# Hybrid encoder layer on one core: the norm's g as a column, applied when transposed tiles leave PSUM, and matmuls of ones ahead of TensorE's first work

## The chip, the cores and the metric

The kernel runs on one core of a Trainium2 chip. The metric is the device time of one execution in microseconds (us). A core has five engines, each with a queue of its own that it works through strictly in order: TensorE (PE in the profile; its weight loads are shown apart as PEld), VectorE (DVE), ScalarE (ACT), GpSimd (POOL) and SyncE (SP), which in this kernel issues most of the transfers. TensorE writes to PSUM, eight banks, which ACT and DVE read; everything else lies in SBUF, 128 partitions wide.

## The reference

One layer of an encoder over x of 1024 tokens by 1024 features, in float32. What matters here is its first step and what uses it:

```python
def rmsnorm(x, g):
    y = x * lax.rsqrt(jnp.mean(x * x, axis=-1, keepdims=True) + EPS)
    return y * g

h = rmsnorm(x, g_mix)
z = h @ w_in                            # pooling channels | q | k | v
y_pool = pool_mixer(z[..., :512], w_pool_grp, pool_scale)
y_attn = diff_attention(q, k, v, ...)   # 8 heads, block-causal
gates = sigmoid(h @ w_gate + b_gate)    # 2048 columns
x = x + (gates[..., :1024] * (y_pool @ w_branch_pool)
         + gates[..., 1024:] * (y_attn @ w_branch_attn)) @ w_out
x = x + square(relu(rmsnorm(x, g_ffn) @ w_up)) @ w_down
```

g_mix has one number for each of the 1024 features. It is 1 plus 0.05 times a normal number, so it can't be left out.

## The kernel before

**Tiles.** The tokens are cut into eight tiles of 128 (t = 0 to 7, x0 to x7). A matmul contracts over the 128 partitions, so h is needed transposed: features on partitions, tokens along the row. hT holds it as eight blocks of 128 features (k = 0 to 7), for each half of the tokens (th = 0, 1), in two parts: a high part, rounded to the format that TensorE takes (float32r), and a low part, the rest. Weights are held in the same two parts. Every product is then three matmuls (`mm3`, L126 to L128: high times high, high times low, low times high), summed in one bank.

**The norm of one tile** (`norm_transpose`, L237) runs over four engines. ACT squares x and sums the rows (L252; for tile 0 ACT and DVE take a half each, L244 and L245); DVE and POOL make the factor rs from the sum (L234 and L235; tile 0: L249 and L250); DVE multiplies x by rs and by g, 512 columns at a time, into hn (L256); TensorE transposes hn, four blocks of 128 into one bank of 512 columns (L261), so that a tile fills two banks, named hps; and `split` brings a bank into hT in two steps of 256 columns each: ACT casts the high part (L120), DVE subtracts it for the low part (L121). On one bank ACT and DVE take turns: ACT's second cast waits for DVE's reading for the first. For L256 g must lie on all 128 partitions: gmb, a tile of 128 by 1024, is loaded by one transfer that repeats the row (L345).

**The order at the start.** `START` (L43) lists the first steps: x0, g, norm of tile 0, four pairs of weights of head 0 (w0 to w3, each two transfers into a tile rqkv; their casts and low parts are made on ACT, POOL and DVE), x1 and so on. SP issues the transfers in that order, all on one queue: x0 in two halves, g, eight transfers of weights, then x1, x2, x3, small parameters, x4. The projection of tile t for head h is named z (`stage_qkv`, L405): eight steps, one per block k, of three matmuls of 384 columns. The other work on TensorE at the start is the first gate block (g in the profile's names, with weights fwgate), 24 matmuls of 512 columns over the first four tiles, and transposes for the heads.

**What sets the order.** A scheduler puts the instructions of each engine in order. It goes by the order in which the code was written, as a priority, and by its own estimate of when each instruction's operands are ready; `tc.issue_after(i)` keeps what is issued under it behind instruction i. So an edit to one step moves others on all engines.

Of the kernel before, what the change touches and what calls it, by code (L numbers as in the profile page):

```python
# [17 lines left out]
P = 128  # L18
# [23 lines left out]

START = "x0 g n0 w0 w1 w2u w3u x1 s0p s1 x2 s2p s3 x3"  # L43
NX = [-2, -1, 0, 0, 0, 1, 2, 3]
# [14 lines left out]
def encoder_kernel(  # L59
# [63 lines left out]
    def mm3(ps, lhs_hi, lhs_lo, rhs_hi, rhs_lo, first, last, more=False):  # L123

        kw = {"skip_group_check": True} if more else {}
        nc.tensor.matmul(ps, lhs_hi, rhs_hi, start=first, stop=False, **kw)  # L126
        nc.tensor.matmul(ps, lhs_hi, rhs_lo, start=False, stop=False, **kw)  # L127
        nc.tensor.matmul(ps, lhs_lo, rhs_hi, start=False, stop=last, **kw)  # L128

# [106 lines left out]

    def norm_transpose(xt, gb, t, dst, hn, small, banks, halves=False):  # L237

# [12 lines left out]
        else:  # L251
            nc.scalar.activation(hn, xt, AF.Square, accum_out=ss)  # L252
            rsq(rs, ss, 1, 1.0 / D)
        for j in range(2):
            js = slice(j * 512, (j + 1) * 512)
            nc.vector.scalar_tensor_tensor(hn[:, js], xt[:, js], rs, gb[:, js], op0=ALU.mult, op1=ALU.mult)  # L256
            trp, trtag = banks[j % len(banks)]
            ps = trp.tile([P, 512], F32, tag=trtag, name=f"hps{t}_{j}")
            for i in range(4):
                k = 4 * j + i  # L260
                nc.tensor.transpose(ps[:, i * P : (i + 1) * P], hn[:, k * P : (k + 1) * P], identf)  # L261
            for i in range(2):
                kp = 2 * j + i
                src = ps[:, i * 256 : (i + 1) * 256].rearrange("p (a b) -> p a b", a=2)
                split(dst[kp, th, 0][:, :, c0 : c0 + P], dst[kp, th, 1][:, :, c0 : c0 + P], src)

# [8 lines left out]
    with ExitStack() as ph:  # L275
# [39 lines left out]
        def norm_x(t):  # L315
# [6 lines left out]
            banks = [(ps_t, "tr"), (ps_s, "sc")][: 2 if t < N_SC else 1]  # L322
            norm_transpose(xs.pop(t), gmb, t, hT, hn, sp, banks, t == 0)

# [7 lines left out]
        KV = {}  # L332
        hT = {}
        for w in START.split():
            if w[0] == "x":
# [5 lines left out]
            elif w[0] == "s":  # L341
                split_w(0, int(w[1]), nc.gpsimd if w[2:] else nc.vector)
            elif w[0] == "g":
                gmb = ut([P, D], F32, "gmb")
                nc.sync.dma_start(gmb, g_mix[0].partition_broadcast(P))  # L345

# [58 lines left out]
        def stage_qkv(h, t):  # L405
# [4 lines left out]
            for k in range(NK):  # L410
                l_hi = hT[k // 2, th, 0][:, k % 2, c0 : c0 + P]
                l_lo = hT[k // 2, th, 1][:, k % 2, c0 : c0 + P]
                w = Wh[h][k]
                mm3(z[:, 0:384], l_hi, l_lo, w[:, 0, :], w[:, 1, :], k == 0, k == NK - 1)
                yield
# [1112 lines left out]
```

## Time and profile before

| | before |
|---|---|
| median of 3 runs | 1529.52 us (1528.83 to 1530.18) |
| the profiled execution | 1529.71 us |
| its span (first to last instruction) | 1527.6 us |
| mean granted TensorE clock | 0.999 |
| instructions | 21675 |
| HBM traffic | 157.76 MB read, 61.90 MB written |

Durations below come from that one execution, so sums are made against its own 1529.71 us: the span and 2.1 us around it. In the profile, each line gives an engine, a line of the kernel, an operation and `out<-in` by the names of the tiles; a time in brackets behind "idle before" is how long the engine had waited, and for whom. The granted clock is a share of TensorE's full clock. "SPq" and "ACTq" are instructions that issue transfers. How the work spreads over the whole span is seen in the page's second part, 40 slices with busy tenths:

```profile
PE   7999999999999999999999999999999999999998
DVE  6776668777777777746578559766665668556572
ACT  6665556656565565454464466555555634333331
POOL 6687333335234242312100011000000000000000
```

A slice is 38 us long. Only the first and the last slice of PE are below 9.

### The profile page before, as it was taken

To read this page: it belongs to the slowest core of one execution; us is meant where nothing else is said; L and a number is where in the kernel's file an instruction comes from. 1 tells how busy PE (TensorE), PEld (TensorE's weight loads), DVE (VectorE), ACT (ScalarE), POOL (GpSimd) and SP (SyncE) were. 2 spreads that over 40 slices of the span, in tenths; PEclk is the share of its full clock that TensorE was granted. 3 is DMA by queue.
4 is the path that set the end of the run, shared out by engine and by line. 5 is a ranking of instruction groups with operands and counts; after the bars stand their busy time and mean duration, and the time that the engine had idled before them with its cause. 6 is when DMAs were issued, how large, how long until landed. Compare 5 with 4: busy or idle time off the path is not lost.

```text
span 1527.6 us, 21675 instructions
## 1 busy us (share of the span) xinstructions
PE 1509.7 (99%) x7441; PEld 1302.0 (85%) x7441; DVE 1048.5 (69%) x2262; ACT 804.7 (53%) x1693; POOL 319.8 (21%) x412
## 2 busy tenths in 40 slices
PE   7999999999999999999999999999999999999998
PEld 6999999999898989888888888888888888888887
DVE  6776668777777777746578559766665668556572
ACT  6665556656565565454464466555555634333331
POOL 6687333335234242312100011000000000000000
PEclk9999999999999999999999999999999999999999
DMA  7253202112112131627365734554433799537750
GB/s 247 100 159 120 76 29 62 51 44 66 43 44 84 49 98 40 223 89 254 120 209 191 248 104 149 169 178 152 148 128 110 274 344 383 170 125 262 228 190 28
DMA packets 171608, 221.07 MB, mean 145 GB/s; under 512 B 10902, under 2 KB 104811, under 8 KB 171499
## 3 DMA queue, kind: packets, MB, share of 16 engines
q1 hardware_dynamic: 154090, 192.39, 38.0%
q10 hardware_dynamic: 17408, 27.30, 4.8%
q8 instruction: 59, 0.97, 0.3%
q14 instruction: 51, 0.41, 0.1%
HBM read 157.76 MB, written 61.90 MB: 144 GB/s over the span
## 4 chain that ended last, share of the span: by engine, by line
PE 95%; DVE 2%; DMA 1%; ACT 1%; SPq 1%; issue 0%; POOL 0%; DVEq 0%
PE z L126 6%; PE z L128 6%; PE z L127 6%; PE Da L126 4%; PE Da L128 4%; PE Da L127 4%; PE g L126 4%; PE g L127 4%; PE g L128 4%; PE Db L126 3%; PE Db L128 3%; PE Db L127 3%; PE X L128 3%; PE X L127 3%; PE X L126 3%; PE sc L484 2%
## 5 line engine op out<-in xcount | busy, mean ns | idle before, releaser
L126 PE MATMUL z<-wqkv,hT 128*128 128x384 f32 x512 | 174.9, 343 | 0.6 <-DVE qn L428 0.4
L128 PE MATMUL z<-wqkv,hT 128*128 128x384 f32 x512 | 173.7, 340 | 0.0
L127 PE MATMUL z<-wqkv,hT 128*128 128x384 f32 x512 | 173.5, 339 | 0.0
L495 ACT ACTIVATE s<-s,nm 128x256 f32<-128x256 f32 (+7 forms) x128 | 99.5, 778 | 46.5 <-DVE nm L487 45.6
L126 PE MATMUL g<-hT,fwgate 128*128 128x512 f32 x256 | 101.1, 395 | 0.1
L127 PE MATMUL g<-hT,fwgate 128*128 128x512 f32 x256 | 100.8, 394 | 0.0
L128 PE MATMUL g<-hT,fwgate 128*128 128x512 f32 x256 | 100.5, 393 | 0.0
L126 PEld LDWEIGHTS z<-wqkv,hT 128*128 128x128 f32 x512 | 96.8, 189 | 3.4 <-DVE qn L428 0.6
L127 PEld LDWEIGHTS z<-wqkv,hT 128*128 128x128 f32 x512 | 96.9, 189 | 3.1 <-POOL wqkv L121 0.2
L235 POOL TENSOR_TENSOR ms<-ms,mhalf 128x4 f32<-128x4 f32 x64 | 65.7, 1027 | 158.3 <-DVE ms L234 135.3
L128 PEld LDWEIGHTS z<-wqkv,hT 128*128 128x128 f32 x512 | 96.5, 189 | 2.5 <-DVE hT L121 0.3
L121 DVE TENSOR_TENSOR AT<-ta,AT 128x256 fp32r<-128x256 f32 (+1 forms) x160 | 62.2, 392 | 32.7 <-ACT AT L120 31.6
L487 DVE CUSTOM_DVE_ANT_0 s<-sc,dist 128x512 f32<-128x512 f32 (+3 forms) x128 | 73.9, 583 | 13.2 <-PE sc L485 12.1
L120 ACT CAST AT<-ta 128x256 fp32r<-128x256 f32 (+1 forms) x160 | 54.5, 347 | 37.9 <-PE ta L527 23.1
L484 PE MATMUL sc<-K,Q 128*128 128x512 f32 (+2 forms) x192 | 69.8, 365 | 0.5 <-DVE nm L487 0.5
L121 DVE TENSOR_TENSOR AS<-s,AS 128x512 fp32r<-128x512 f32 x64 | 44.1, 693 | 36.5 <-ACT AS L120 36.3
L485 PE MATMUL sc<-K,Q 128*128 128x512 f32 (+2 forms) x192 | 66.4, 350 | 0.0
L121 POOL TENSOR_TENSOR wqkv<-rqkv,wqkv 128x384 fp32r<-128x384 f32 x60 | 61.8, 1044 | 19.8 <-ACT wqkv L120 16.7
L121 POOL TENSOR_TENSOR fwgate<-frgate,fwgate 128x512 fp32r<-128x512 f32 x32 | 43.3, 1356 | 66.0 <-ACT fwgate L120 66.0
L126 PEld LDWEIGHTS g<-hT,fwgate 128*128 128x128 f32 x256 | 48.1, 188 | 9.3 <-ACT go L730 0.5
L128 PEld LDWEIGHTS g<-hT,fwgate 128*128 128x128 f32 x256 | 48.1, 188 | 8.9
L127 PEld LDWEIGHTS g<-hT,fwgate 128*128 128x128 f32 x256 | 48.1, 188 | 8.4
(455 smaller groups left out, 4485.0 us busy)
## 6 DMA issues: line engine op xcount, KB each, us to landing
wd<-in_w_down_dram SPq DMA_DIRECT2D x56, 512.0 KB, 5.6
wu<-in_w_up_dram SPq DMA_DIRECT2D x32, 512.0 KB, 4.4
udS<-us SPq DMA_DIRECT2D x64, 256.0 KB, 2.4
ur<-udS SPq DMA_DIRECT2D x32, 512.0 KB, 3.4
rqkv<-in_w_in_dram SPq DMA_DIRECT2D x64, 192.0 KB, 2.7
ud<-u ACTq DMA_DIRECT2D x48, 256.0 KB, 4.1
ur<-ud SPq DMA_DIRECT2D x24, 512.0 KB, 4.3
frgate<-in_w_gate_dram SPq DMA_DIRECT2D x32, 256.0 KB, 2.8
```

Of the source, the lines that this page charges most:

```text
L120: nc.scalar.copy(hi, src)
L121: return (lo_eng or nc.vector).tensor_tensor(lo, src, f(hi), op=ALU.subtract)
L126: nc.tensor.matmul(ps, lhs_hi, rhs_hi, start=first, stop=False, **kw)
L127: nc.tensor.matmul(ps, lhs_hi, rhs_lo, start=False, stop=False, **kw)
L128: nc.tensor.matmul(ps, lhs_lo, rhs_hi, start=False, stop=last, **kw)
L235: nc.gpsimd.tensor_tensor(dst, dst, mhalf[:, :n], op=ALU.pow)
L484: nc.tensor.matmul(dst, Q[:, i, 0, :], rhs, start=True, stop=False)
L485: nc.tensor.matmul(dst, Q[:, i, 1, :], rhs, start=False, stop=True)
L487: nc.vector.tensor_tensor_reduce(out=s[i][:, c : c + w], in0=sc[:, 0:w], in1=dist[:, o0 + c : o0 + c + w], scale=2.0 ** -(h + 1), scalar=B ...
L495: nc.scalar.activation(s[i][:, 0:n], s[i][:, 0:n], AF.Exp, bias=last, scale=-1.0, accum_out=Z[:, i, t : t + 1])
```

## The change

g is no longer multiplied into hn. It is loaded as a tile of 8 rows by 128 (grow; ACT issues the transfer), transposed by TensorE into a bank and copied by DVE to gcol, one column of 128 for each block k. DVE's multiply makes hn from x and rs alone (`tensor_scalar`). When a transposed block leaves its bank, its features lie on partitions, so g is a number per partition: ACT's copy takes gcol as its scale and gives the high part, and DVE's `scalar_tensor_tensor` takes the bank times gcol, less the high part. This is done for each block of 128 columns apart: eight pieces on ACT and eight on DVE for a tile, where there were four and four. The large transfer of g is gone from SP's queue.

The squares of tiles 1 to 3 on ACT are held behind an earlier tile's last piece (`cast_done`: tile 0's for tiles 1 and 2, tile 1's for tile 3). And TensorE multiplies a tile of ones by itself, 512 columns, into a bank that nobody reads (idle): 16 times ahead of everything else, and 4 times behind the last matmul of z of tile 0.

```diff
-START = "x0 g n0 w0 w1 w2u w3u x1 s0p s1 x2 s2p s3 x3"
+START = "x0 n0 w0 w1 w2u w3u x1 s0p s1 x2 s2p s3 x3"
...
-        nc.tensor.matmul(ps, lhs_lo, rhs_hi, start=False, stop=last, **kw)
+        return nc.tensor.matmul(ps, lhs_lo, rhs_hi, start=False, stop=last, **kw).ins
...
-            nc.scalar.activation(hn, xt, AF.Square, accum_out=ss)
+            with ExitStack() as behind:
+                if t < 4:
+                    behind.enter_context(tc.issue_after(cast_done[0 if t < 3 else 1]))
+                nc.scalar.activation(hn, xt, AF.Square, accum_out=ss)
             rsq(rs, ss, 1, 1.0 / D)
         for j in range(2):
             js = slice(j * 512, (j + 1) * 512)
-            nc.vector.scalar_tensor_tensor(hn[:, js], xt[:, js], rs, gb[:, js], op0=ALU.mult, op1=ALU.mult)
+            nc.vector.tensor_scalar(hn[:, js], xt[:, js], rs, None, op0=ALU.mult)
...
-            for i in range(2):
-                kp = 2 * j + i
-                src = ps[:, i * 256 : (i + 1) * 256].rearrange("p (a b) -> p a b", a=2)
-                split(dst[kp, th, 0][:, :, c0 : c0 + P], dst[kp, th, 1][:, :, c0 : c0 + P], src)
+            for i in range(4):
+                k, src = 4 * j + i, ps[:, i * P : (i + 1) * P]
+                hi, lo = (dst[k // 2, th, d][:, k % 2, c0 : c0 + P] for d in range(2))
+                cast_done[t] = nc.scalar.activation(hi, src, AF.Copy, scale=gcol[:, k : k + 1]).ins
+                nc.vector.scalar_tensor_tensor(
+                    lo, src, gcol[:, k : k + 1], f(hi), op0=ALU.mult, op1=ALU.subtract
+                )
...
+        idle = ps_o.tile([P, 512], F32, tag="o", name="idle")
+
+        def keep_warm(n):
+            for _ in range(n):
+                nc.tensor.matmul(
+                    idle.rearrange("p (a b) -> p a b", a=4), ones, ones.unsqueeze(1).broadcast_to([P, 4, P]),
+                    start=True, stop=True,
+                )
+
+        keep_warm(16)
+        gcol = sp.tile([P, NK], F32, name="gcol")
+        grow = sp.tile([NK, P], F32, name="grow")
+        nc.scalar.dma_start(grow, g_mix[0].rearrange("(k p) -> k p", p=P))
+        g_ps = ps_t.tile([P, 512], F32, tag="tr", name="g_ps")
+        nc.tensor.transpose(g_ps[:, 0:NK], grow, identf[0:NK, 0:NK])
+        nc.vector.tensor_copy(gcol, g_ps[:, 0:NK])
...
-            elif w[0] == "g":
-                gmb = ut([P, D], F32, "gmb")
-                nc.sync.dma_start(gmb, g_mix[0].partition_broadcast(P))
...
-                mm3(z[:, 0:384], l_hi, l_lo, w[:, 0, :], w[:, 1, :], k == 0, k == NK - 1)
+                done = mm3(z[:, 0:384], l_hi, l_lo, w[:, 0, :], w[:, 1, :], k == 0, k == NK - 1)
+                if (h, t, k) == (0, 0, NK - 1):
+                    with tc.issue_after(done):
+                        keep_warm(4)
```

How the scheduler's order moves is seen at two places. The first is ACT's first tile: the casts of the eight weight halves of head 0 (wqkv from rqkv) and the high parts of hT of tile 0, from the banks hps0_0 (blocks 0 to 3) and hps0_1 (blocks 4 to 7). hT0 to hT3 are pairs of blocks; the next number of the name is the half of the tokens and the one after it 0 for the high part. Before:

```order
L120 CAST wqkv0_0_200<-rqkv0_0_186 128x384
L120 CAST wqkv0_1_203<-rqkv0_0_186 128x384
L120 CAST wqkv0_2_206<-rqkv0_1_189 128x384
L120 CAST hT0_0_0_150<-hps0_0_167 128x2x128
L120 CAST wqkv0_3_209<-rqkv0_1_189 128x384
L120 CAST wqkv0_4_214<-rqkv0_2_192 128x384
L120 CAST hT2_0_0_154<-hps0_1_177 128x2x128
L120 CAST hT1_0_0_152<-hps0_0_167 128x2x128
L120 CAST wqkv0_5_217<-rqkv0_2_192 128x384
L120 CAST wqkv0_6_220<-rqkv0_3_195 128x384
L120 CAST hT3_0_0_156<-hps0_1_177 128x2x128
```

And of the change, from the third weight half on:

```order
L120 CAST wqkv0_2_235<-rqkv0_1_218 128x384
L120 CAST wqkv0_3_238<-rqkv0_1_218 128x384
L120 CAST wqkv0_4_243<-rqkv0_2_221 128x384
L120 CAST wqkv0_5_246<-rqkv0_2_221 128x384
L270 ACTIVATE hT0_0_0_171<-hps0_0_188,gcol_162 128x128
L120 CAST wqkv0_6_249<-rqkv0_3_224 128x384
L270 ACTIVATE hT2_0_0_175<-hps0_1_202,gcol_162 128x128
L120 CAST wqkv0_7_252<-rqkv0_3_224 128x384
L270 ACTIVATE hT0_0_0_171<-hps0_0_188,gcol_162 128x128
L270 ACTIVATE hT2_0_0_175<-hps0_1_202,gcol_162 128x128
L270 ACTIVATE hT1_0_0_173<-hps0_0_188,gcol_162 128x128
L270 ACTIVATE hT3_0_0_177<-hps0_1_202,gcol_162 128x128
```

The first piece of hT stood behind three weight casts and stands behind six now; the pieces of the two banks alternate behind them.

The second place is PE behind z of tile 0 (z0_0; z0_1 is tile 1's). Before:

```order
L127 MATMUL z0_0_372<-wqkv0_7_223,hT3_0_0_156 128x384
L128 MATMUL z0_0_372<-wqkv0_7_223,hT3_0_1_157 128x384
L261 MATMUL hps1_0_255<-identf_96,hn1_248 128x128 x4
L261 MATMUL hps1_1_265<-identf_96,hn1_248 128x128 x4
L126 MATMUL z0_1_442<-wqkv0_0_200,hT0_0_0_150 128x384
L127 MATMUL z0_1_442<-wqkv0_0_200,hT0_0_0_150 128x384
L128 MATMUL z0_1_442<-wqkv0_0_200,hT0_0_1_151 128x384
```

And of the change:

```order
L127 MATMUL z0_0_433<-wqkv0_7_252,hT3_0_0_177 128x384
L128 MATMUL z0_0_433<-wqkv0_7_252,hT3_0_1_178 128x384
L346 MATMUL idle_145<-ones_103 128x512 x4
L266 MATMUL hps1_0_284<-identf_96,hn1_277 128x128 x4
L266 MATMUL hps1_1_298<-identf_96,hn1_277 128x128 x4
L266 MATMUL hps2_0_322<-identf_96,hn2_315 128x128 x4
L126 MATMUL z0_1_515<-wqkv0_0_229,hT0_0_0_171 128x384
```

Four matmuls of ones stand between z of tile 0 and tile 1's transposes, and half of tile 2's transposes have moved ahead of z of tile 1. On DVE the multiply of tile 3 by its factor now stands behind the making of tile 4's factor, and tile 3's transposes stand ahead of z of tile 2 on PE.

More of the change, by code (lines that the diff above doesn't have):

```diff
@@ L235, in rsq, with norm_transpose @@
         nc.gpsimd.tensor_tensor(dst, dst, mhalf[:, :n], op=ALU.pow)
-    def norm_transpose(xt, gb, t, dst, hn, small, banks, halves=False):
+    cast_done = {}
+    def norm_transpose(xt, gcol, t, dst, hn, small, banks, halves=False):
         th, c0 = t // 4, (t % 4) * P
@@ L322, in norm_x @@
             banks = [(ps_t, "tr"), (ps_s, "sc")][: 2 if t < N_SC else 1]
-            norm_transpose(xs.pop(t), gmb, t, hT, hn, sp, banks, t == 0)
+            norm_transpose(xs.pop(t), gcol, t, hT, hn, sp, banks, t == 0)
         def split_w(h, kp, eng):
```

## Prediction

> **What bounds the kernel now.** First the page's busy shares and the waits of PE over the whole span (engine, line, whom it waited for: us, times, longest).
>
> ```profile
> PE 1509.7 (99%) x7441; PEld 1302.0 (85%) x7441; DVE 1048.5 (69%) x2262; ACT 804.7 (53%) x1693; POOL 319.8 (21%) x412
> PE hps L261 <- DVE hn L256: 10.6, 2, 8.8
> ```
>
> TensorE is the bound: it is idle for 1527.6 - 1509.7 = 17.9 us, and 10.6 of these are two waits of the norm's transposes, 8.8 at the start and 1.8 later. The change works on the norm, so the question is how much of the first 43 us it can win. Second view: the windows (length, then busy us of PE, PEld, DVE, ACT, POOL, then granted clock, DMA share, GB/s).
>
> ```profile
> 0.00:8.75 8.75, 0.00 (x0) 0.00 (x0) 1.72 (x5) 2.29 (x4) 2.25 (x27) 1.00 0.76 211
> 8.75:15.86 7.11, 7.11 (x32) 6.09 (x32) 5.00 (x9) 5.58 (x14) 5.07 (x4) 1.00 0.98 329
> 15.86:17.66 1.80, 0.00 (x1) 0.03 (x1) 1.05 (x3) 1.46 (x4) 0.56 (x1) 1.00 0.71 168
> 17.66:22.10 4.44, 4.44 (x20) 3.96 (x21) 4.22 (x15) 3.43 (x9) 3.57 (x5) 0.62 0.81 263
> 22.10:42.92 20.82, 20.82 (x127) 19.32 (x125) 18.78 (x47) 14.41 (x39) 13.01 (x17) 1.00 0.57 181
> ```
>
> From 22.10 on PE is full at full clock, so nothing that comes later can be won by starting work earlier, except through this start. Its losses are: 8.75 idle; a slow first projection (z of token tile 0, 8.75 to 15.86); 1.80 idle; and 17.66 to 22.10 at a mean clock of 0.62, which costs 4.44 x 0.38 = 1.7 us. Third view: the timeline, for what each loss waits on (start, us, engine, line, instruction; in brackets the idle time before and who ended it).
>
> ```profile
> 5.40 0.57 POOL L250 TENSOR_TENSOR rs<-rs,mhalf 128x1 f32<-128x1 f32 x1 [3.16 <-DVE rs L249]
> 7.95 1.41 DVE L256 SCALAR_TENSOR_TENSOR hn<-x,rs,gmb 128x512 f32<-128x512 f32 x2 [2.70 <-DMA gmb<-in_g_mix_dram]
> 8.47 1.62 ACT L120 CAST wqkv<-rqkv 128x384 fp32r<-128x384 f32 x3 [4.17 <-DMA rqkv<-in_w_in_dram]
> 11.22 0.53 PE L128 MATMUL z<-wqkv,hT 128*128 128x384 f32 x1
> 11.55 0.48 PE L126 MATMUL z<-wqkv,hT 128*128 128x384 f32 x1
> 12.04 0.34 PE L128 MATMUL z<-wqkv,hT 128*128 128x384 f32 x1
> 12.22 0.35 PE L126 MATMUL z<-wqkv,hT 128*128 128x384 f32 x1
> 14.75 1.06 ACT L252 ACTIVATE hn<-x 128x1024 f32<-128x1024 f32 x1 [1.44 <-DMA x<-in_x_dram]
> ```
>
> Token tile 0's factor is ready at 5.97, but its multiply waits for g (gmb) until 7.95. The first weights land at 8.47 only. Matmuls of one shape start 0.33 apart at 11.2 and 0.18 at 12.0: the first 3 us ran at half clock, though the window says 1.00. The 1.80 gap waits for x1, which lands at 14.75 behind the weights.
>
> **The change, part by part.**
>
> *g leaves the queue.* The transfer of g and the rate around it:
>
> ```profile
> gmb<-in_g_mix_dram SPq DMA_DIRECT2D x1, 512.0 KB, 6.2
> 3.00:4.00 1.00, 0.00 (x0) 0.00 (x0) 0.00 (x0) 0.43 (x1) 0.00 (x0) 1.00 1.01 236
> 4.00:5.00 1.00, 0.00 (x0) 0.00 (x0) 0.70 (x2) 0.29 (x2) 0.00 (x0) 1.00 0.86 160
> 6.00:7.00 1.00, 0.00 (x0) 0.00 (x0) 0.00 (x0) 0.00 (x0) 0.00 (x0) 1.00 1.00 321
> 12.39 0.55 SPq L356 DMA_DIRECT2D gqk<-in_g_k_dram  x1
> SPq L356 <- DMA rqkv<-in_w_in_dram: 0.2, 1, 0.2
> ```
>
> While g moves, the rate is 160 GB/s; with weights alone 321 and more. 512 KB at these rates are 3.3 and 1.6 us; I take 2.75 (nearer the first, since the slow stretch is 3.4 to 6). The eight half-transfers of the weights land from 8.47 to about 12.38 (SP's wait for the last), 0.56 apart; afterwards from 5.7 to 9.6, the sixth at 8.5. x1 lands at 14.75 - 2.75 = 12.0. The new transfer of g is 4 KB, issued by ACT before its table load, while ACT has nothing to do until 3.57; it costs nothing.
>
> *The first tile on ACT.* The order of ACT (above) is decisive: the pieces of hT now stand behind the casts of all first six weight halves, so the first piece starts no earlier than 8.5 + 0.5 = 9.0, although its transposes could be ready at 6.0 + 0.4 + 0.5 = 6.9. The pieces' costs, from rows of other work (busy us, mean ns):
>
> ```profile
> L120 ACT CAST V<-z 128x128 fp32r<-128x128 f32 x64 | 15.7, 267 | 0.0
> L722 ACT ACTIVATE yps<-yp,cols 128x512 f32<-128x512 f32 x8 | 5.5, 686 | 0.4 <-PE yp L128 0.2
> L1272 ACT COPY z<-Z 128x512 f32<-128x512 f32 x16 | 9.4, 588 | 10.1 <-PE Z L128 9.2 <-ACT u L1248 0.9
> L121 DVE TENSOR_TENSOR V<-z,V 128x128 fp32r<-128x128 f32 x64 | 17.8, 278 | 0.0
> L121 DVE TENSOR_TENSOR AS<-s,AS 128x512 fp32r<-128x512 f32 x64 | 44.1, 693 | 36.5 <-ACT AS L120 36.3
> L256 DVE SCALAR_TENSOR_TENSOR hn<-x,rs,gmb x15: 737/746/1781, 7.9 to 39.4; 128x512 f32<-128x512 f32 x15
> 31.11 0.90 ACT L120 CAST hT<-hps 128x256 fp32r<-128x256 f32 x3
> L120 ACT CAST hT<-hps 128x256 fp32r<-128x256 f32 x32 | 11.0, 374 | 4.3 <-PE hps L261 3.8 <-DVE hT L121 0.2
> ```
>
> A column as scale adds 686 - 588 = 98 ns, so an ACT piece takes 0.36 us; casts in a row overlap by 0.374 - (0.90 - 0.374) / 2 = 0.11, so pieces in a row stand 0.25 to 0.26 apart. A DVE piece takes 278 + (746 - 693) = 0.33. One bank is read by ACT and DVE in turn, 0.36 + 0.33 + two handovers of some 0.05 = 0.8 a piece; two banks give 0.4 a piece. With the last two weight casts (0.5 each) among them, eight pieces last 0.36 + 1.0 + 0.36 + 6 x 0.4 = 4.1: the last low part is there at 9.0 + 4.1 + 0.1 = 13.2. PE does the first four of z's eight steps as pieces come (to 13.1), and then 12 matmuls: 12 x 0.175 = 2.1 at full clock, 12 x 0.32 = 3.8 at half. z ends at 15.2 to 16.9, against 15.86.
>
> *Multiplying ones.*
>
> ```profile
> 0.90 0.20 POOL L218 MEMSET ones<- 128x128 f32 x1
> 31.61 0.40 PE L127 MATMUL g<-hT,fwgate 128*128 128x512 f32 x1
> 31.84 0.39 PE L128 MATMUL g<-hT,fwgate 128*128 128x512 f32 x1
> ...
> 18.00:19.00 1.00, 1.00 (x8) 0.72 (x7) 1.00 (x7) 0.37 (x1) 0.62 (x2) 0.84 0.84 332
> 20.00:21.00 1.00, 1.00 (x5) 0.90 (x4) 1.00 (x3) 1.00 (x4) 0.92 (x2) 0.50 0.87 244
> ```
>
> The ones are set at 1.10. Sixteen matmuls of 512 columns, 0.23 apart at full clock and some 0.45 at half, end between 6.4 and 8.4: off the path, since the first piece is not read before 9.0. Do they keep the clock up until 13.1? From 8 to 13 PE has some 2 us of work in 5, and in the last two rows 1.80 us without work were enough to bring the clock to 0.50. I therefore take half the tail as slow: z ends at 16.0. The Trainium skill ("TensorE: Matmul & The Clock Gate", section "Why this matters for your kernels") asks only that gaps between bursts stay under some 3 us; the trace speaks against it, 1.80 us did harm. By the page z would end at 15.2.
>
> The four extra matmuls behind z lie on the path: 4 x 0.23 to 0.45 = 0.9 to 1.8; I take 1.0. x1's square stands behind tile 0's last piece on ACT (12.9); with 1.06 for it, 0.15 and 0.57 for the factor and two multiplies of 0.4 x1 is ready at about 15.6, covered by z. So x1's transposes start at 17.0 (16.1 to 18.7) instead of 17.66: **gain 0.66**. Since PE has no gap of 1.8 us ahead of them now, I count them and what follows at full clock: **gain 1.7** (bounds 0 and 1.7).
>
> *Tiles 1 to 4.* ACT and DVE must bring hT while PE works at full clock.
>
> ```profile
> 17.11:34.14 17.03, 16.48 (x93) 15.42 (x94) 15.65 (x43) 14.13 (x38) 13.28 (x18) 0.90 0.82 263
> L1037 DVE TENSOR_SCALAR gfb<-gfb 128x1024 f32<-128x1024 f32 x1 | 0.7, 695 | 4.5 <-DMA gfb<-in_g_ffn_dram 4.5
> ```
>
> ACT has 17.03 - 14.13 = 2.9 us free here; the gate's matmuls at 31.61 use tile 3's hT while ACT is still writing it (31.11), so an ACT that is later makes PE wait. Four tiles swap 16 casts, 0.265 apart, for 32 pieces, 0.26 apart: + 4.1 us, 1.2 beyond the free time. Two places in the order add a little: hn of x3 stands behind x4's factor on DVE, and the second tile's first piece stands ahead of the rest of the first tile's: 0.45 together. **Loss 1.65.** Bounds: 0 if pieces follow 0.16 apart, 4.9 at 0.36 (no overlap at all). DVE's multiply gets cheaper (half of 695 and a start, 0.36 to 0.43, for 0.75), its pieces dearer (8 x 0.26 for 4 x 0.33): + 0.2 a tile, in 1.4 us free. Tiles 5 to 7 come after 35, where ACT has room.
>
> Sum: 0.66 + 1.7 - 1.65 = 0.7 us gained. The profiled execution took 1529.71 (span 1527.6 and 2.1 around it; the median shown is 1529.52): **1529.0**.
>
> **Rivals.**
> 1. *It keeps up.* z ends at 15.2, the four matmuls cost 0.9, no stall follows: 1.56 + 1.7 = 3.3, with up to 1 from the rest of the new order: 1525.5. For it: pieces wait for no transfer after 9.6. Against: the 0.8 a bank, and ACT's order.
> 2. *ACT becomes the bound and the clock falls again* (the slower side). If pieces stand 0.36 apart, PE idles in several places between 18 and 34, and as at 18 to 22 the clock falls: 0.66 + 0 - 4.9 = 4.2 us slower, 1533.9; without the clock's gain it is over 0.2% slower from 0.33 a piece on (32 x 0.33 - 4.2 - 2.9 + 0.45 = 3.9 lost), with the worst start from 0.27. The chain of a bank (0.8) speaks for it, the overlap of casts against it.
> 3. *The clock holds through the short gaps*, 1.80 having been too long but 0.4 not: z ends at 15.2 and, with the losses above, 1528.1. Against: too little work from 8 to 13. That the ones do not do what they are for, before z, is in the forecast already.
>
> **How the numbers follow.** Forecast 0.43, rival 1 0.27, rival 2 0.16, rival 3 0.14. Within 0.2% (3.06 us, about what a measurement of this kernel tells from no change) lie the forecast and rival 3: 0.57; faster 0.27; slower 0.16. The range runs from rival 1's 1525.5 to the worst start without rival 2's stalls: 18.7 at x1's transposes (1.04 lost), no clock gain, 1.65 lost: 1532.4.
>
> **What would show it.** Right: the timeline has ACT's first hT piece at 9.0, z's end near 16.0, x1's transposes near 17, a granted clock of 1.00 from 17 to 22, and waits of PE for hT or hn of 1 to 2 us in all between 18 and 36. Wrong: z before 15, no wait of PE behind it (rival 1); PE waits over 3 us or a clock of 0.50 after 20 (rival 2).

## The result, and the profile after

| | before | after |
|---|---|---|
| median (6 runs each) | 1529.41 us (1528.35 to 1530.18) | 1539.49 us (1537.30 to 1540.79) |
| the profiled execution, its span | 1529.71 us, 1527.6 us | 1539.38 us, 1537.6 us |
| mean granted TensorE clock | 0.999 | 0.998 |

After is slower: ratio 1.0065, 95% interval 1.0052 to 1.0078, some 10 us. The prediction, 1529.0 in a range from 1525.5 to 1532.4, was wrong.

First the windows of after, cut where TensorE's state changes (length, then busy us of PE, PEld, DVE, ACT, POOL, granted clock, DMA share, GB/s):

```profile
7.54:13.04 5.50, 3.31 (x16) 1.96 (x16) 4.77 (x11) 4.20 (x12) 2.60 (x3) 1.00 1.01 364
13.04:16.46 3.42, 3.42 (x12) 3.34 (x13) 2.09 (x8) 2.75 (x7) 1.14 (x2) 0.50 0.66 208
16.46:25.63 9.17, 8.74 (x52) 7.55 (x51) 6.21 (x25) 6.73 (x21) 3.89 (x7) 1.00 0.96 306
25.63:30.11 4.48, 1.46 (x9) 0.84 (x8) 4.48 (x6) 4.48 (x13) 4.06 (x5) 1.00 0.62 226
30.11:33.52 3.41, 3.24 (x12) 3.24 (x13) 2.83 (x13) 2.91 (x7) 2.26 (x4) 0.50 0.24 68
33.52:48.40 14.88, 14.88 (x86) 13.50 (x84) 11.69 (x35) 8.32 (x27) 5.18 (x7) 1.00 0.12 36
60.00:100.00 40.00, 38.63 (x211) 34.30 (x210) 29.73 (x79) 23.02 (x63) 32.24 (x46) 1.00 0.50 157
100.00:200.00 100.00, 98.75 (x558) 90.61 (x558) 74.88 (x237) 59.19 (x158) 58.24 (x80) 1.00 0.33 108
```

Before was full at full clock from 22.10 on. After has a hole from 25.63 to 30.11, in which ACT and DVE are busy throughout and TensorE for a third, then a second stretch of half clock; and it loses 1.37 us between 60 and 100 and 1.25 between 100 and 200, where nothing of the norm runs. Now the timeline of the hole, TensorE first, then ACT and DVE (start, us, engine, line, instruction, idle time before and who ended it):

```profile
25.46 0.34 PE L128 MATMUL z<-wqkv,hT 128*128 128x384 f32 x1
26.34 0.63 PE L266 MATMUL hps<-identf,hn 128*128 128x128 f32 x4 [0.54 <-ACT V L120]
27.66 0.66 PE L266 MATMUL hps<-identf,hn 128*128 128x128 f32 x4 [0.70 <-DVE hn L261]
30.28 1.11 PE L266 MATMUL hps<-identf,hn 128*128 128x128 f32 x4 [1.96 <-DVE hT L271]
31.05 0.67 PE L126 MATMUL z<-wqkv,hT 128*128 128x384 f32 x1
```
```profile
19.24 3.84 ACT L270 ACTIVATE hT<-hps,gcol 128x128 fp32r<-128x128 f32 x13 [0.89 <-PE hps L266]
22.92 1.11 ACT L257 ACTIVATE hn<-x 128x1024 f32<-128x1024 f32 x1
23.96 1.11 ACT L257 ACTIVATE hn<-x 128x1024 f32<-128x1024 f32 x1
```
```profile
25.45 0.35 DVE L271 SCALAR_TENSOR_TENSOR hT<-hps,gcol,hT 128x128 fp32r<-128x128 f32 x1
25.72 4.26 DVE L261 TENSOR_SCALAR hn<-x,rs 128x512 f32<-128x512 f32 x4
29.90 0.33 DVE L271 SCALAR_TENSOR_TENSOR hT<-hps,gcol,hT 128x128 fp32r<-128x128 f32 x1
30.35 0.41 DVE L452 TENSOR_TENSOR qn<-z,ms 128x256 f32<-128x256 f32 x1
```

Tile 2's projection (z, 31.05) stands on TensorE behind the transposes of tile 3 (26.34, 27.66) and half of tile 4's (30.28). Tile 3's wait for the multiplies of x3 on DVE; tile 4's wait for a bank that DVE's low part at 29.90 sets free, behind all four multiplies (25.72 to 29.98). z waits for DVE in one more way: there are two banks for z, so tile 2's takes over that of tile 0, which DVE reads last for qn, at 30.35 to 30.76, behind the same multiplies. The multiplies wait for the squares of x3 and x4 on ACT (22.92, 23.96), and those came behind thirteen pieces of hT in a row (19.24 to 23.08). Before, x3's square started at 19.27:

```profile
19.27 1.06 ACT L252 ACTIVATE hn<-x 128x1024 f32<-128x1024 f32 x1
```

No single wait of TensorE is over 2 us; the queues of ACT, DVE and TensorE, each in strict order, pass the delay on.

The losses can be counted. Below, every matmul but those of ones counts as much as its usual distance to the next one of its shape (0.174 us for 384 columns, 0.227 for 512, 0.118 for 256, 0.108 to 0.110 for 128, the median in before). The first row is when before had done that much work; the others are how many us later (+) or earlier (-) a kernel got there in its profiled execution:

| work done, us | 10 | 20 | 30 | 60 | 100 | 300 | 600 | 1400 |
|---|---|---|---|---|---|---|---|---|
| before, at | 24.59 | 34.57 | 45.11 | 75.30 | 115.80 | 318.29 | 623.75 | 1426.91 |
| after | 0.0 | +5.5 | +6.6 | +6.8 | +9.9 | +10.9 | +10.0 | +10.3 |
| ones_on_before | -0.6 | +0.6 | +0.6 | +0.5 | +0.5 | +0.5 | +0.6 | +0.9 |
| no_ones | -0.2 | +7.0 | +9.4 | +10.5 | +11.1 | +10.8 | +10.9 | +10.8 |
| hold_first | +5.0 | +6.1 | +7.4 | +8.1 | +8.7 | +8.8 | +12.4 | +12.5 |
| column_only | +0.2 | +0.4 | +1.2 | +1.9 | +2.4 | +2.5 | +6.2 | +6.5 |
| column_far_order | -1.4 | +5.0 | +7.4 | +7.6 | +7.5 | +7.2 | +7.2 | +7.1 |
| pieces_on_before | +4.2 | +5.3 | +6.0 | +5.9 | +5.7 | +6.7 | +6.8 | +8.2 |
| wide_after | -1.9 | -1.2 | -1.2 | -1.3 | -1.2 | -1.4 | -3.6 | -3.4 |
| wide_no_ones | -2.5 | -1.9 | -1.8 | -1.8 | -1.9 | -2.2 | -2.2 | -2.4 |
| act_wide | -2.9 | -2.2 | -1.3 | -1.3 | -0.1 | +0.7 | +2.5 | +2.8 |
| dve_wide | +0.3 | +1.2 | +1.4 | +1.5 | +1.2 | +2.3 | +4.2 | +4.2 |
| act_wide_far_order | -4.1 | -3.2 | -1.3 | 0.0 | -0.1 | +0.1 | +0.1 | 0.0 |

Each row is one execution and can lie up to 3 us from its kernel's median (no_ones 1540.35 against 1537.59, column_far_order 1536.64 against 1533.67). After has 5.5 us of its loss by 40 us, 1.1 more by 52, 3.1 between 82 and 126 and 0.6 elsewhere.

### The profile page after: what moved, and what is told of

Its sections match the earlier page's. It is cut to its first block, busy times and chain, and to the rows that moved or that the text cites. A ratio compares the mean times of both kernels' runs of the same rounds, so it can differ in the third digit from the quotient of the medians.

```text
span 1537.6 us, 21799 instructions
## 1 busy us (share of the span) xinstructions
PE 1519.8 (99%) x7462; PEld 1307.8 (85%) x7462; DVE 1052.2 (68%) x2295; ACT 815.1 (53%) x1725; POOL 317.1 (21%) x412
## 4 chain that ended last, share of the span: by engine, by line
PE 94%; DVE 3%; DMA 1%; ACT 1%; issue 1%; SPq 0%; DVEq 0%; ACTq 0%
PE z L126 6%; PE z L128 6%; PE z L127 6%; PE g L126 4%; PE Da L126 4%; PE Da L127 4%; PE Da L128 4%; PE g L127 4%; PE g L128 4%; PE Db L127 3%; PE Db L126 3%; PE Db L128 3%; PE X L128 3%; PE X L126 3%; PE X L127 3%; PE sc L508 2%
## 5 line engine op out<-in xcount | busy, mean ns | idle before, releaser
L511 DVE CUSTOM_DVE_ANT_0 s<-sc,dist 128x512 f32<-128x512 f32 (+3 forms) x128 | 74.3, 583 | 11.9 <-PE sc L509 11.1
L121 POOL TENSOR_TENSOR wqkv<-rqkv,wqkv 128x384 fp32r<-128x384 f32 x60 | 62.3, 1056 | 10.3 <-ACT wqkv L120 9.3
```

What stands on the lines that cost most here:

```text
L121: return (lo_eng or nc.vector).tensor_tensor(lo, src, f(hi), op=ALU.subtract)
L511: nc.vector.tensor_tensor_reduce(out=s[i][:, c : c + w], in0=sc[:, 0:w], in1=dist[:, o0 + c : o0 + c + w], scale=2.0 ** -(h + 1), scalar=B ...
```

## Experiments

Seventeen kernels ran beside before and after, one of them (g_by_tensore) for a second profile. Medians are set against the median of before measured on the same chip beside them; ratios have their 95% interval.

**Hold, ones or pieces?** Four kernels take the change apart.

```diff
# hold_first: after, with
-                    behind.enter_context(tc.issue_after(cast_done[0 if t < 3 else 1]))
+                    behind.enter_context(tc.issue_after(cast_done[0]))
# no_ones: after, without keep_warm(16) and keep_warm(4)
# column_only: no_ones, and no issue_after on the squares
# ones_on_before: before, with keep_warm(16) and keep_warm(4) at the same places
```

hold_first: 

> After, with one index changed: x3's square (the row tile's sum of squares on ACT) waits for the last piece of tile 0, as x1's and x2's do, and not for that of tile 1. Theory H (the hold): TensorE stands idle from 25.6 to 31.05 because x3's square starts at 22.92 instead of 19.27 as before, behind every piece of tiles 1 and 2 on ACT, and the transposes of tiles 3 and 4 stand ahead of tile 2's z on TensorE; with the hold moved, tile 2's z begins by about 27, the second stretch of half clock (1.7 us) goes too, and the time falls by 4 to 6 us to 1533 to 1536. Theory O (the ones): the matmuls of ones are what costs; the time stays within 1 us of 1539.5. Theory P (the pieces): sixteen small operations on ACT and on DVE for each row tile are too slow for TensorE whatever the order; the stall moves to other places and the time stays above 1537.

Measured 1540.60 us, ratio 1.0075 (1.0062 to 1.0087): not faster than after. Theory H in this form falls.

no_ones: 

> After without any matmul of ones (neither the sixteen at the start nor the four behind tile 0's z); g's column, the pieces and the holds on the squares stay. Theory H: the stall ahead of tile 2's z stays, 1538 to 1541, or a little less where the four ones (0.9 us in row) go from the path. Theory O: back to 1530 to 1533. Theory P: 1537 to 1540. In all of them the first stretch of half clock, at 13.0 to 16.5 with the ones, moves: without ones the clock has to be watched from 9 to 22.

Measured 1537.59, ratio 1.0056 (1.0043 to 1.0069). Theory O falls: 1.9 us less than after, not 6 or more.

column_only: 

> After without ones and without any hold on the squares: what is left is g as a column, applied by eight pieces on ACT and eight on DVE per row tile. Theory H: near before, 1528 to 1533. Theory O: the same as no_ones within 1 us. Theory P: 1535 to 1540, with TensorE waiting for pieces (ACT hT, DVE hT) more than 3 us between 18 and 45.

Measured 1536.16, ratio 1.0043 (1.0031 to 1.0056): inside P's numbers, but not by P's mechanism alone. By the table it is only 1.9 us late at 77 us and loses 3.7 between 321 and 630.

ones_on_before: 

> The kernel before with the ones alone: sixteen ahead of the first work and four behind tile 0's z; g stays a row of 1024 on all partitions, multiplied into hn. Theory O: slower than before by 2 us or more. Theories H and P: between 1.7 us faster (the stretch of half clock at 18.7 to 22.1 goes) and 1 us slower (the four ones, 0.93 us, lie on the path), so 1527.7 to 1530.5.

Measured 1529.14 against 1529.47, ratio 0.9998 (0.9989 to 1.0008): no difference. TensorE's order is that of before there, and its row in the table stays level from 30 us on. The ones remove the slow stretch at 18.7 and bring one at 12.0 instead:

```profile
8.00:16.00 8.00, 6.14 (x25) 5.18 (x26) 6.23 (x11) 6.60 (x15) 4.70 (x5) 0.79 1.03 346
16.00:25.00 9.00, 8.97 (x54) 8.00 (x53) 7.91 (x23) 6.59 (x18) 5.03 (x9) 1.00 0.94 279
```

These are windows of ones_on_before; before has a clock of 1.00 and 0.81 in the same two rows. (Its first 3 us at half clock, which the prediction read from the spacing of the matmuls, do not show in the granted clock.)

**The order far away, and the pieces alone.** The scheduler's order was compared between kernels. hold_first and column_only share one order of TensorE from some 50 us on, but for five rows, and it is not that of before; both lose 3.6 to 3.7 us between the work of 300 and 600. So:

```diff
# column_far_order: column_only, with
+                if t in {4: 3}:
+                    behind.enter_context(tc.issue_after(cast_done[3]))
# pieces_on_before: before, with a bank drained in four
-            for i in range(2):
-                kp = 2 * j + i
-                src = ps[:, i * 256 : (i + 1) * 256].rearrange("p (a b) -> p a b", a=2)
-                split(dst[kp, th, 0][:, :, c0 : c0 + P], dst[kp, th, 1][:, :, c0 : c0 + P], src)
+            for i in range(4):
+                k, src = 4 * j + i, ps[:, i * P : (i + 1) * P]
+                split(dst[k // 2, th, 0][:, k % 2, c0 : c0 + P], dst[k // 2, th, 1][:, k % 2, c0 : c0 + P], src)
```

column_far_order: 

> column_only with one hold: x4's square on ACT waits for the last piece of tile 3. Near the change TensorE's order stays that of column_only but for a few transposes; from row 1000 of TensorE's order on (about 200 us) it is that of before again, but for 73 rows, where column_only has 3654 rows moved in rows 1000 to 3500. Theory F (the order far from the change): of column_only's 6.7 us some 3.1 are lost between 310 and 420 us, where nothing of the norm runs, because the scheduler put far work in another order; here they are not lost, 1532 to 1534. Theory P (the pieces cost what they cost, wherever it shows): 1535 to 1537.

Measured 1533.67 (1531.74 to 1536.64, a wide spread; the profiled execution was the longest), ratio 1.0028 (1.0016 to 1.0039). That is theory F's range. From 52 us on its row stays level (+7.4, +7.1), so with before's far order nothing is lost far away; but the one hold moved the near order and lost 7 us there. The near part was not held fixed as intended.

pieces_on_before: 

> The kernel before with each bank drained in four steps of 128 columns instead of two of 256, on ACT and on DVE; g stays a row, no ones, no holds. Theory P: the smaller pieces make TensorE wait 3 us or more between 17 and 45, 1533 to 1536. Theory F: near the change less than 1.5 us are lost; TensorE's order is another one from row 2000 on (3199 rows moved), which can cost or gain some 3 us there, so 1528 to 1534, and the account of lost time by stretch shows it at places far from the norm.

Measured 1536.55 against 1529.78, ratio 1.0046 (1.0033 to 1.0059). That is half a microsecond above theory P's range. Smaller steps alone, with nothing else of the change, cost 6.0 us by 51 us; the scheduler's order near the norm moves with them. TensorE's waits of pieces_on_before between 7 and 60 us (who waited for whom: us, times, longest):

```profile
PE z L128 <- DVE hT L121: 2.1, 2, 1.7
PE z L126 <- ACT hT L120: 1.3, 2, 0.8
```

The wait of 1.7 us, at 25.3 to 27.0, is for a low part that stands on DVE behind the four multiplies of x3 and x4, as in after:

```profile
23.82 2.94 DVE L256 SCALAR_TENSOR_TENSOR hn<-x,rs,gmb 128x512 f32<-128x512 f32 x4
```

It is followed there, too, by half clock (27.7 to 31.1).

**The head start without pieces.** g can leave SP's queue in other ways.

```diff
# g_on_act_queue: before, with
-                nc.sync.dma_start(gmb, g_mix[0].partition_broadcast(P))
+                nc.scalar.dma_start(gmb, g_mix[0].partition_broadcast(P))
# g_by_tensore: before without that transfer, and ahead of START
+        nc.scalar.dma_start(gmb[0:1, :], g_mix[0:1])
+        for j, (pool, tag) in enumerate([(ps_t, "tr"), (ps_s, "sc")]):
+            g_ps = pool.tile([P, 512], F32, tag=tag, name=f"g_ps{j}")
+            nc.tensor.matmul(g_ps, f(ones)[0:1, :], gmb[0:1, j * 512 : (j + 1) * 512], start=True, stop=True)
+            (nc.scalar.copy, nc.vector.tensor_copy)[j](gmb[:, j * 512 : (j + 1) * 512], g_ps)
# row_by_tensore_8_ones: g_by_tensore, with keep_warm(8) ahead of it
```

g_on_act_queue: 

> The kernel before with one word changed: g's transfer of 512 KB is issued on ACT's queue instead of SP's, so that weights and x1 do not stand behind it. Theory G (the head start is worth something): tile 0's multiply and x1's transposes come up to 2 us earlier, 1527 to 1529. Theory F: TensorE's order moves far away too (1929 rows between 2000 and 3500), which by itself can move the time by 3 us either way, 1528 to 1533, whatever the start gains.

Measured 1539.02, ratio 1.0062 (1.0050 to 1.0074). One word, and 9 us slower, outside both theories: 2.8 us late at 10 us of work, 5.4 at 300, 8.3 at 1400. Part of the first loss shows: g now moves beside x0, whose second half lands at 7.01 where DVE had it at 4.22 before, so tile 0's transposes start at 10.34 instead of 8.75. The rest was not followed further.

g_by_tensore: 

> The kernel before with g's row loaded on one partition only (4 KB, ACT's queue) and laid on all partitions by two matmuls with a row of ones; ACT and DVE copy the two banks to gmb. Nothing else changes: g is multiplied into hn as before, banks are drained in steps of 256. Theory G: the start of after without pieces, so tile 0's multiply starts at 6.0 instead of 7.95, weights and x1 come 2.75 us earlier, and the end 1 to 2.5 us earlier, 1527 to 1528.5. Theory F: the far order is another one again (1419 rows between 2000 and 3500), 1526 to 1533.

Measured 1532.19, ratio 1.0016 (1.0007 to 1.0025), in two groups of six runs each: theory F's range, not G's.

row_by_tensore_8_ones: 

> g_by_tensore with eight matmuls of ones ahead of the first work. TensorE's order is that of before, instruction for instruction, from row 250 on (about 45 us), so no far loss can come from the order itself. Theory G: the start, with g's 512 KB gone and wide drains, is worth 1 to 2.5 us: 1527 to 1528.5. Theory C (the clock eats it): TensorE starts earlier, but in small bursts between waits, and runs at half clock for some 3 us longer than before; the time is within 1 us of before.

Measured 1533.03 against 1529.28, ratio 1.0028 (1.0017 to 1.0040). Neither: in its profiled execution, the shortest of seven, it is 2.1 us late by 37 us, with one wait of 2.2 us ahead of 28.8 for a low part of hT, and level after that.

g_by_tensore_again: 

> The same kernel as g_by_tensore, for a second profile: its twelve times fall into two groups, 1529.2 to 1530.6 and 1533.8 to 1535.2, and the profiled one was of the second. In that one a DVE operation on one column (cf, L506) took 4.61 us at 86.56, while GpSimd ran without a pause from 83.4 to 91.6. Theory L (DVE waits for a pause of GpSimd): in a run of the first group this operation takes 0.2 to 1.3 us and TensorE does not wait for it; in one of the second group it is again over 4 us. Rival: the groups differ at another place.

One execution, 1530.25. The row in question on DVE, first of g_by_tensore and then of g_by_tensore_again:

```profile
86.56 4.61 DVE L506 SCALAR_TENSOR_TENSOR cf<-cf,Z,nlam 128x1 f32<-128x1 f32 x1
```
```profile
87.87 0.37 DVE L506 SCALAR_TENSOR_TENSOR cf<-cf,Z,nlam 128x1 f32<-128x1 f32 x1
```

The times are as theory L said. In the first TensorE waited 2.92 us and had 3.4 us of half clock behind it (91.8 to 95.2); the second has neither. After has the same event. The reason that theory L gave does not hold, though. GpSimd of g_by_tensore_again:

```profile
87.49 0.74 POOL L769 TENSOR_TENSOR wq<-wq 128x256 f32<-128x256 f32 x1
88.18 2.58 POOL L121 TENSOR_TENSOR wqkv<-rqkv,wqkv 128x384 fp32r<-128x384 f32 x2
```

There was no pause here either; DVE's operation ended at 88.24, as one GpSimd instruction ended (88.23) and the next followed. Why DVE got its turn at 88.24 in this run, and in the other only at 91.18, where GpSimd paused for 0.09 us, stays open.

**The size of the pieces within after.** The four that decide:

```diff
# wide_after: after, with a bank drained in two
+            for i in range(2):
+                k, src = 4 * j + 2 * i, ps[:, i * 256 : (i + 1) * 256].rearrange("p (a b) -> p a b", a=2)
+                hi, lo = (dst[k // 2, th, d][:, :, c0 : c0 + P] for d in range(2))
# wide_no_ones: the same edit in no_ones
# act_wide: after, with ACT in two and DVE in four
+                cast_done[t] = nc.scalar.copy(hi2, src2).ins
+                for b in range(2):
+                    nc.vector.scalar_tensor_tensor(
+                        lo2[:, b], src2[:, b], gcol[:, k + b : k + b + 1], f(hi2[:, b]), op0=ALU.mult, op1=ALU.subtract
+                    )
# dve_wide: the mirror image, ACT in four and DVE in two
```

wide_after: 

> After with half the pieces: ACT and DVE drain a bank in two steps of 256 columns, with one column of gcol for both blocks. Left out: every second block's own g (the first block's is used), so only the time counts. Ones and holds stay, and TensorE's order stays that of after up to tile 2's z: tile 3's transposes and half of tile 4's still stand ahead of it. Theory P (pieces): the wait ahead of tile 2's z shrinks from 4 us to under 1.5 and the time falls to 1532 to 1535. Theory H2 (the hold with TensorE's strict order: x3's square comes late whatever the size of the pieces): a wait of 3 us or more stays at 24 to 31, and the time stays above 1536.

Measured 1525.89 against 1529.28, ratio 0.9975 (0.9966 to 0.9984): 13.6 us less than after, faster than before, and 6 us below theory P's range. ACT, DVE and TensorE of wide_after at the place of the hole:

```profile
20.77 1.08 ACT L257 ACTIVATE hn<-x 128x1024 f32<-128x1024 f32 x1
```
```profile
23.09 0.88 DVE L261 TENSOR_SCALAR hn<-x,rs 128x512 f32<-128x512 f32 x2
24.81 1.09 DVE L261 TENSOR_SCALAR hn<-x,rs 128x512 f32<-128x512 f32 x2
```
```profile
23.57 0.34 PE L128 MATMUL z<-wqkv,hT 128*128 128x384 f32 x1
23.75 1.04 PE L266 MATMUL hps<-identf,hn 128*128 128x128 f32 x8
24.95 0.44 PE L126 MATMUL z<-wqkv,hT 128*128 128x384 f32 x1 [0.16 <-DVE qn L452]
```

x3's square comes 2.15 us earlier than in after, its multiply 2.6 earlier, and the four multiplies take 1.97 us instead of 4.26. Of these 4.26 most lie beside GpSimd's work on the gate's weights (POOL in after):

```profile
26.00 2.73 POOL L121 TENSOR_TENSOR fwgate<-frgate,fwgate 128x512 fp32r<-128x512 f32 x2
```

So the pieces made the multiplies late by 2.6 us, that brought them beside GpSimd, and there they took 2.3 us more. TensorE goes from z to the transposes and on without a hole. One thing was not as expected: the scheduler's order near the change moved with the steps. Half of tile 4's transposes, ahead of tile 2's z in after, stand behind it here; and x4's multiplies, ahead of qn on DVE in after, stand behind it (qn at 24.48, the multiplies at 24.81). So a part of the hole (28.3 to 31.05) went by the order.

wide_no_ones: 

> no_ones (1537.6) with half the pieces, as in wide_after; the first block's g is used for two blocks. Its far order is that of before from row 2000 on, as that of no_ones. Theory P: 1531 to 1534. Theory H2: above 1535, with tile 3's transposes waiting for their multiply near 25 as in no_ones (3.7 us there).

Measured 1527.29, ratio 0.9988 (0.9979 to 0.9997): 10.3 us less than no_ones, and again below theory P's range. In this pair TensorE's order speaks the other way: no_ones has half of tile 3's transposes ahead of tile 2's z, wide_no_ones all of them, and still the wait of 3.7 us is gone. ACT's order moved as well. In no_ones a cast of the gate's weights, which waits for its transfer, stands between the pieces and x3's square:

```profile
23.91 0.62 ACT L120 CAST fwgate<-frgate 128x512 fp32r<-128x512 f32 x1 [1.24 <-DMA frgate<-in_w_gate_dram]
24.95 1.06 ACT L257 ACTIVATE hn<-x 128x1024 f32<-128x1024 f32 x1
```

In wide_no_ones x3's square is at 20.16 and that cast behind it, at 24.06. The size of the steps is all that was edited in both pairs, so it is the cause of the 13.6 and 10.3 us. How much of them came by longer rows of steps and how much by the order that the scheduler then chose was not separated. With steps of 256 the holds on the squares, which are in this kernel too, cost nothing that shows.

act_wide: 

> After with ACT draining 256 columns at a time and DVE 128 as in after. ACT's high part is the rounded bank without g; DVE's low part is the bank times its own column less that, so high plus low is still h, with a low part as large as h times (g - 1). Theory A (ACT's sixteen small steps per tile pair are the cost): near wide_after, 1526 to 1529. Theory D (DVE's are): near after, 1536 to 1540. Theory B (both, through the bank on which they take turns): in between, 1531 to 1535.

Measured 1531.04 against 1529.30, ratio 1.0014 (1.0005 to 1.0023).

dve_wide: 

> The mirror image: ACT in pieces of 128, DVE in steps of 256, each with the first block's column for both blocks, so every second block's own g is left out. Theory A: 1536 to 1540. Theory D: 1526 to 1529. Theory B: 1531 to 1535.

Measured 1532.35, ratio 1.0021 (1.0012 to 1.0030). Both halves win 7 to 8.5 of the 13.6 us, as theory B said. In the table the near part of act_wide is no worse than wide_after's (-2.2 at 32 us, with no half clock behind the matmuls of ones); what it lacks is lost later, between 74 and 626 us.

**Versions with the right g everywhere.**

```diff
# g_in_weights: wide_after with plain casts of hT; g goes to the weights, e.g.
+                    nc.scalar.activation(w[:, 0, :], rw[:, i, :], AF.Copy, scale=gk)
+                    eng.scalar_tensor_tensor(w[:, 1, :], rw[:, i, :], gk, f(w[:, 0, :]), op0=ALU.mult, op1=ALU.subtract)
...
+            for kk in range(4):
+                nc.scalar.activation(rw[:, kk, :], rw[:, kk, :], AF.Copy, scale=gcol[:, 4 * j + kk : 4 * j + kk + 1])
# column_tile0_g_late: pieces with gcol for t == 0 only, else as before; keep_warm(16), no keep_warm(4); holds for t < 3
+START = "x0 n0 w0 w1 w2u w3u x1 g s0p s1 x2 s2p s3 x3"
# column_tile0_g_mid: the same without holds, and
+START = "x0 n0 w0 w1 w2u w3u g x1 s0p s1 x2 s2p s3 x3"
# act_wide_far_order: act_wide, with keep_warm(12) and without keep_warm(4)
```

g_in_weights: 

> wide_after with g taken to the weights: hT is the normed x without g, drained by 256 with plain casts, and the weights of q, k, v, pooling channels and gates, whose features also lie on partitions, are multiplied by gcol on ACT before they are split (56 more steps of 128x384, about 0.56 us each, and 160 of 128x128, 0.27 apart: some 74 us on ACT, which is busy 805 of 1528 us). Nothing is left out. If ACT hides them: 1524.5 to 1528. If ACT's extra work near the start delays the weights of head 0 or the first gate block: 1529 to 1534.

Measured 1553.37, ratio 1.0157 (1.0140 to 1.0175), far outside: 5.6 us late at 10 us of work, 11.1 at 100, 22.5 at 600. ACT did the extra work as counted (880.8 us busy against 804.7 before). Near the start it was not hidden: by 60 us TensorE waits 4.2 us for ACT's hT and weights, and it runs at half clock from 12.3 to 22.6. The later losses were not taken apart.

column_tile0_g_late: 

> g as a column for tile 0 alone (eight pieces on ACT and DVE); tiles 1 to 7 as before, with g's row on 128 partitions, whose transfer is now issued behind x1's; sixteen matmuls of ones, no four; the squares of x1 and x2 wait for tile 0's last piece. TensorE's order is that of before throughout. Theory B (pieces of tiles 1 to 4 are the loss, tile 0's are nearly free): 1526.5 to 1529. Rival (tile 0's pieces cost too, or g's transfer of 512 KB only moves the wait to x1 or x2): 1529 to 1532.

Measured 1529.20 against 1529.53, ratio 0.9997 (0.9988 to 1.0006).

column_tile0_g_mid: 

> The same with g's row issued behind the weights and ahead of x1, and without holds. TensorE's order is that of before throughout. Theory B: 1527 to 1529; x1 lands as late as before (near 14.75), so the gain is smaller than in column_tile0_g_late by up to 1 us. Rival: 1529 to 1532.

Measured 1530.24, ratio 1.0005 (0.9996 to 1.0013). With the pieces on tile 0 alone, and TensorE's order that of before, the time is that of before: what after loses hangs on tiles 1 to 7 and the order that comes with their pieces. But both lie in the rival's range: the head start brings nothing that lasts there either.

act_wide_far_order: 

> act_wide with twelve matmuls of ones instead of sixteen and without the four behind tile 0's z, which lets the scheduler end in before's order of TensorE from row 2000 (about 410 us) on, with 255 rows moved in rows 1000 to 2000 where act_wide has 660 and 2727. Theory F (the far order costs act_wide some 4 us): 1526 to 1528.5, faster than before and after. Rival (the small pieces of DVE cost that much themselves, everywhere): 1530 to 1532 again.

Measured 1529.22 against 1529.47, ratio 0.9999 (0.9990 to 1.0008). Half of theory F holds: from 75 us on nothing is lost any more (0.0 at 60 us of work, 0.0 at 1400), where act_wide lost 4.1. But of its lead of 4.1 us at 20.5 us, all is gone by 75, 1.7 of it in a stretch of half clock from 43.1 to 46.5 behind three short waits between 39.9 and 42.7, the longest 0.68 us, for hT of the later tiles. The time misses both ranges, between them. No version with every block's own g beat before.

## Why the prediction was wrong

**g leaves the queue: right in kind.** ACT's first piece was forecast at 9.0 and came at 9.38. It started right behind the cast of the sixth weight half, which ended at 9.35 (forecast 9.0). DVE's copy of gcol, behind low parts of weights, was done at 9.28, hardly ahead of it.

```profile
9.13 0.15 DVE L357 COPY gcol<-g_ps 128x8 f32<-128x8 f32 x1
9.38 0.37 ACT L270 ACTIVATE hT<-hps,gcol 128x128 fp32r<-128x128 f32 x1
```

**z of tile 0: 16.0 forecast, 17.7 measured.** The pieces kept TensorE at 3.31 us of work in 5.50 (the first window above), and the clock fell to 0.50 at 13.04 for 3.4 us. The forecast had 12 of the 24 matmuls done by 13.1 and half of the other 12 slow; in fact 7 had started by then, since the last low part came at 14.26 and not at 13.2, and 11 ran slowly. Five more to do at 0.174 and five more slow ones at 0.146 extra are 1.6 of the 1.7 us. x1's transposes started at 18.61, not 17.0: instead of 0.66 gained, 0.95 were lost. The four matmuls of ones took 0.93, as forecast at 1.0.

**The gain of 1.7 from the clock: held until 30.11, then lost.** The granted clock is 1.00 from 16.46 to 30.11 as forecast, and 0.50 from 30.11 to 33.52, behind the hole.

**The step that failed: "Tiles 1 to 4 … Loss 1.65".** The pieces were priced well: 0.37 us on ACT (forecast 0.36), 0.35 on DVE (0.33), and 13 in a row stand (3.84 - 0.37) / 12 = 0.29 apart (0.26). The step failed in what it did with the prices. It set ACT's added busy time against ACT's free time in 17 us, as if work could be moved freely within them. What counted was the way through the queues: pieces, then x3's square, then its multiply, then its transposes, and tile 2's z behind those. By 40 us the loss was 5.5 in all. With 0.95 lost at x1's transposes and 1.7 gained from the clock, the term itself was 5.5 - 0.95 + 1.7 = 6.25 us, 1.7 of it the second stretch of half clock, where the forecast had 1.65 with an upper end of 4.9. (With steps of 256 there is a gain of 1.2 at the same point.) That the size of the pieces is the cause is shown by wide_after and wide_no_ones, and from the other side by pieces_on_before. Their price hangs on the order: without holds and ones column_only has lost 0.4 us at the same point, with the holds no_ones 7.0, and pieces_on_before 5.3 without either; with wide steps the holds cost nothing.

"Tiles 5 to 7 come after 35, where ACT has room" was not free either: 1.1 us went by 52 us, in two waits of TensorE for DVE (0.37 ahead of 49.09, 0.66 ahead of 50.16).

ACT still had its free time (the window of after that the prediction showed of before; ACT is the fourth busy time):

```profile
17.11:34.14 17.03, 13.41 (x72) 11.60 (x71) 13.49 (x40) 14.12 (x39) 10.24 (x15) 0.90 0.71 230
```

14.12 us against 14.13: an engine with 2.9 us free was late all the same.

**A term that was missing: the order far from the change.** The prediction counted nothing behind 35 us, since TensorE was full there. Full can't be improved, but it can be broken. After lost 3.1 us between 82 and 126, in two waits for DVE. The first, with 2.1 us of the loss, stands behind one DVE operation on a single column, which took as long as GpSimd worked without a pause (DVE, then POOL of after, then TensorE's waits between 48 and 200 us):

```profile
93.05 5.07 DVE L527 SCALAR_TENSOR_TENSOR cf<-cf,Z,nlam 128x1 f32<-128x1 f32 x1
```
```profile
92.92 0.75 POOL L790 TENSOR_TENSOR wq<-wq 128x256 f32<-128x256 f32 x1
93.61 2.00 POOL L121 TENSOR_TENSOR wqkv<-rqkv,wqkv 128x384 fp32r<-128x384 f32 x2
95.56 0.47 POOL L458 TENSOR_TENSOR qn<-qn,ggh 128x128 f32<-128x128 f32 x1
95.97 0.75 POOL L785 CAST wd<-wq 128x256 fp32r<-128x256 f32 x2
96.67 0.74 POOL L790 TENSOR_TENSOR wq<-wq 128x256 f32<-128x256 f32 x1
97.36 0.74 POOL L802 TENSOR_TENSOR wq<-wq 128x256 f32<-128x256 f32 x1
98.19 0.38 POOL L421 TENSOR_SCALAR ggh<-gg 128x64 f32<-128x64 f32 x1
```
```profile
PE ta L551 <- DVE s L528: 2.5, 2, 1.4
```

GpSimd's instructions follow each other until 98.10 and the next starts at 98.19; DVE's ends at 98.12. Its like at 106.65 took 0.22; the second wait follows there, and whether the first brought it on was not tried. The two profiles of g_by_tensore show the same with and without the event, 4 us apart in time; they are one kernel with one order, so this event is a matter of timing, which an earlier delay can shift. How often it comes in after is not known. That a far order can cost 3 us or more is further shown by hold_first and column_only (+3.6 and +3.7 in the same order), and that before's far order costs nothing by column_far_order and act_wide_far_order. The 13.6 us between after and wide_after and the 3.4 us of wide_after against before therefore hold such shares too: of the 3.4, 1.4 are there at 300 us of work and the rest comes between 300 and 600.

**The rivals.** Rival 2 was the nearest: TensorE idles between 18 and 34 and the clock falls again. Its condition, pieces 0.36 apart, was not met (0.29), and its price of 4.9 was less than the 6.25. ACT was not the bound by its busy time, as it said, but by its place in a chain. Rival 1's sign came with wider steps, but not by its path: z of tile 0 ended near 16.9 in wide_after, not at 15.2. Rival 3 was wrong: the clock didn't hold.

## What to carry to other kernels

Cutting a step in two on an engine with free time isn't priced by that free time: follow what stands behind it in each queue up to the next thing that the busiest engine needs, and price the first wait that this brings there, with the slow clock behind it. Where a scheduler orders the whole program, a small edit is also a new order far away, worth 2 to 4 us either way here; compare when the same amount of work was done before blaming the edit. To test a part, look for a variant whose order elsewhere is that of the kernel before.

## What the hardware showed that was not expected

- A DVE operation on one column, 0.22 us where GpSimd left room, took 5.07 in after and 4.61 in g_by_tensore, and in after it ended when GpSimd paused. The Trainium skill ("SBUF — State Buffer", section "🔬 SBUF: two separate sides") says that a DVE operation with two SBUF inputs and a GpSimd operation that reads SBUF exclude each other for a whole instruction. The traces agree that DVE stands still. In g_by_tensore_again it did so for one instruction (0.37 us, to 88.24); in after it stood still for eight GpSimd instructions in a row. Which of the two comes was not settled.
- DVE's multiply without g, 0.48 us alone, took up to 1.50 beside GpSimd's work; four of them 4.26 instead of 1.97.
- The slow clock came in stretches of 3.41 us and its multiples, up to 10.24 (g_in_weights at 12.32). One came behind a single wait of 1.80 us (before), others behind thin work without a long wait: 5.5 us at 60% busy (after at 13.04), 3.46 us at 63% busy (act_wide_far_order at 43.06). But a wait of 2.15 us, with 1.26 us of work in 3.41, was followed by none (row_by_tensore_8_ones, 25.40 to 28.81). So the length of one wait does not tell.
